# The FFN down products of a streaming trunk step: from fp32r halves to scaled float16 halves

## The chip, the cores and the metric

The kernel runs on one core of one Trainium2 chip, as one program. The metric is the device time of an execution in microseconds; the profile of one execution gives the time of each instruction on TensorE (matmuls and their weight loads), VectorE, ScalarE, GpSimd and on the DMA queues.

## The reference, cut to what matters

One layer (`DEPTH` 1) over 2048 prompt frames and 64 sample frames, 2112 tokens of width 1024: a mixer (gated delta rule and pooling), then a SwiGLU feed-forward network of width 2816, each with a residual addition, and a final norm. The change is about the last product, by `w_down`, and about the operands of it.

```python
def hybrid_layer(x, ...):
    h = rmsnorm(x, norm1_w)
    ...                                   # mixer: o_delta, o_pool and the new states
    x = x + jnp.concatenate([o_delta, o_pool], axis=-1) @ w_out
    h = rmsnorm(x, norm2_w)
    x = x + (jax.nn.silu(h @ w_gate) * (h @ w_up)) @ w_down
    return x, ...
D_FF = -(-8 * D_MODEL // (3 * 256)) * 256   # 2816 = 22 tiles of 128
```

## The kernel before

**Order of the work.** The program writes every operation down in an order of its own; a list scheduler inside it (`Machine`) then simulates the five engines with its own costs and issues each engine's instructions in the order that the simulation found. An operation's rank is its place in the program, lowered by `boost` (`hurry` lowers by `HURRY`, for the operations that read PSUM). The engines run what they were given in that order. Tiles are slots of a tag with a number of buffers, handed out in the simulation; PSUM has eight banks, and the tag "mm" has three (`PSM`). Loads and stores go through SP's queue.

**Mixer.** Four blocks of 512 tokens (the first has the 64 sample frames too), up to about 936 us. Between its weights the plan has steps `("pre", "dn", f0, m)`, 16 of them in blocks 1 to 3: `pre_sums` loads two tiles of `w_down`, forms the Strassen sums on GpSimd, splits each into two fp32r halves and stores them in `dsd`.

**Feed-forward network.** Three blocks of 704 tokens (`NB2`, two halves of `N2` = 352). The 22 f tiles (128 features each) lie in groups of `FGROUPS` = 4, 4, 4, 4, 2, 4. For each block and f tile, `gate_up` makes gate and up as one Strassen product (seven products x, y, z of 12 matmuls, operands as pairs of float16 halves, each product from hi x hi, hi x lo and lo x hi), and leaves silu(gate) * up as a raw tile "hr" of two halves of tokens. Its weights are scaled for each f tile from the data (`scale_of`: sum of squares over the partitions by matmuls of width 1 with ones, then a power of two), split in block 0, stored (`gsd`) and loaded in blocks 1 and 2.

Every second f tile, `factors` makes the seven right factors of the Strassen down product from a pair of raw tiles: four additions on GpSimd (VectorE for the last pair) and seven splits into fp32r halves, a ScalarE cast and a VectorE subtract each, in a tile of tag "op" (two buffers, 13 x 352) and one of tag "h7". `down_strassen` runs a group: for each of four pairs of output tiles m (two for the group of two) seven products of `len(hs)` x 3 matmuls, each added by VectorE into two of the tiles `ys` straight from PSUM. The names of its PSUM tiles in the profile are dx, dy and dz; hq is a factor, wsd and wsdS are weights, wrd the raw weights. Its weights come from `load_down` (sums from `dsd`, the plain quarters loaded raw and split) or, where no sums were stored, from `prep_down` (raw load, sums on GpSimd, four splits). `PRE` says which groups have stored sums in which block.

Plain products, d in the profile, take the place of Strassen's for groups 0 and 4 of block 0 and for the last group of block 2 (the latter in two halves of tokens, so that the last norm can begin); they stay fp32r, before and after, with tiles h3l of the tag "op".

The list `order` says when a group's down work comes: after tile f0 + G for most groups, one tile later for group 0 and, in block 0, for groups 1 to 3 (`LATER`, `LATE0`); for the last group after the last tile. Between the blocks the chain `between` normalises the block just done, loads the next `ys` and makes the next inputs, which `load_h` brings in (hA, hB, hBT).

Of the kernel before, what the change touches and what calls it, by code (L numbers as in the profile page):

```python
# [18 lines left out]
P = 128  # L19
# [33 lines left out]
LATE0 = (1,2,3)  # L53
# [11 lines left out]
class Machine:  # L65
# [124 lines left out]
    def issue(self):  # L190
# [180 lines left out]
def hybrid_kernel(ctx, tc, a, o):  # L371
# [124 lines left out]
    n1w, n2w, nfw = (nw[:, i * KT : (i + 1) * KT] for i in range(3))  # L496
    ones_b = cpool.tile([P, P], BF16, tag="onesb", name="onesb")
# [17 lines left out]
    def weigh_norm():  # L515

        sq = cpool.tile([P, 4], F32, tag="sq", name="sqn", bufs=2)
        junk = cpool.tile([P, KT], F32, tag="junkn", name="junkn")
        act(junk, n2w, AF.Square, accum_out=sq[:, :1])
# [4 lines left out]
    groups, f0 = [], 0  # L524
    for G in FGROUPS:
        groups.append((f0, G))
        f0 += G
    plan, pres = [], []
    for gi, (f0, G) in enumerate(groups):
        pres += [("pre", "gu", f, i) for f in range(f0, f0 + G) if f in PRE_GU for i in range(2)]  # L530
        pres += [("pre", "dn", f0, m) for m in range(KT // 2) if gi in PRE[0]]
# [10 lines left out]
    for j in range(NBLK):  # L542
# [5 lines left out]
        else:  # L548
# [12 lines left out]
    gpd = {(f, i): dpool.tile([4, P, 512], F32, tag=f"gpd{f}_{i}", name=f"gpd{f}_{i}") for f in PRE_GU for i in range(2)}  # L561

# [8 lines left out]
    for b in range(NB2):  # L571
        for f in range(NF):
            order.append(("gu", b, f))
            order += [("dn", b, gi) for gi, (f0, G) in enumerate(groups) if f == min(f0 + G + LATER * (gi == 0 or b == 0 and gi in LATE0), NF - 1)]
    for op in order:
        if op[0] == "gu":
            plan.append(("gu", op[2]))
        else:
            plan += [("dn", m, *groups[op[2]]) for m in range(KT)] * len(halves(*op[1:])) if plain(*op[1:]) else [
                ("ds", m, *groups[op[2]], op[2] in PRE[op[1]]) for m in range(KT // 2 * groups[op[2]][1] // 4)]  # L580
# [16 lines left out]
    def prep():  # L597
        key = plan[state["at"]]
        state["at"] += 1
        if key[0] == "pre":  # L600
            return pre_sums(*key[1:])
        if key in stored and key[0] != "gu":
# [32 lines left out]
        elif key[0] == "ds":  # L635
            parts = load_down(*key[1:4]) if key[4] else prep_down(*key[1:4])
# [4 lines left out]
        while due and due[0][0] != key:  # L641
# [3 lines left out]
            stored.add(k)  # L645

    def prep_strassen(key):
# [16 lines left out]
        junk = wq["pool"].tile([P, 512], BF16, tag="junk", name=f"junk{f}")  # L664
# [28 lines left out]
    def pre_sums(what, f, i):  # L693

        n = 256
        (tl, tr), (ll, lr) = ([t[:, i * n : i * n + n] for i in range(2)] for t in (
            names["poolw"], gp.tile([P, PX], F32, tag="pw", name=f"pr{what}{f}_{i}", bufs=2)[:, :512]))
        if what == "dn":
            for t, m0 in ((tl, i), (ll, i + KT // 2)):
                both = bass.AP(t.tensor, t.offset, [list(t.ap[0]), [1, 2 * n]])  # L700
                nc.sync.dma_start(out=both, in_=a["wd"][m0][:, f * P : f * P + 2 * n])
            dst = dsd[f, i]
        else:
            for t, nm, at in ((tl, "wg", 0), (tr, "wg", 512), (ll, "wu", 0), (lr, "wu", 512)):
                nc.sync.dma_start(out=t, in_=a[nm][f][:, at + i * n : at + i * n + n])
            dst = gpd[f, i]
        gt = nc.gpsimd.tensor_tensor
        spare = B.spare + B.o_spare + (prev.o_spare if prev else [])
# [9 lines left out]
    def split_w(t, x):  # L718

        nc.scalar.copy(t[:, 0], x)  # L720
        tt(t[:, 1], x, t[:, 0].bitcast(F32), ALU.subtract)

    def load_down(m, f0, G):

        n, t = G // 2 * P, {}
        for i, nms in enumerate((("11", "12"), ("S3", "S1"), ("S2", "S4"), ("22",))):
            raw, part = wtiles(f"d{nms[0]}", i % 2 == 1)
            part = part()
            if nms[0][0] == "S":
                both = part.rearrange("p q n -> p (q n)").rearrange("p (j q n) -> p j q n", j=2, q=2)  # L730
                nc.sync.dma_start(out=both.rearrange("p j q n -> p j (q n)").bitcast(F32),
                                  in_=dsd[f0, m][2 * i - 2 : 2 * i].rearrange("j p n -> p j n"))
                t |= {nm: [both[:, j]] for j, nm in enumerate(nms)}
            else:
                raw, k = raw(), n * len(nms)
                src = a["wd"][m + (KT // 2 if i else 0)]
                nc.sync.dma_start(out=raw[:, :k], in_=src[:, (f0 + G) * P - k : (f0 + G) * P])
                wsplit(part, raw, k)
                t |= {nm: [part[:, :, j * n : j * n + n]] for j, nm in enumerate(nms)}
        return t  # L740

    def prep_down(m, f0, G):

        n, M = G // 2 * P, 4 // G
# [3 lines left out]
        for t, m0 in ((top, m * M), (low, m * M + KT // 2)):  # L748
            nc.sync.dma_start(out=parts(t), in_=a["wd"][m0 : m0 + M, :, f0 * P : (f0 + G) * P].rearrange("m p c -> p m c"))
# [6 lines left out]
        t = {}  # L756
        for i, (nms, raw) in enumerate(((("11", "12"), top), (("S3", "S1"), s31), (("S2", "S4"), s24), (("22",), low))):
            part = wtiles(f"d{nms[0]}", i % 2 == 1)[1]()
            if len(nms) == 2:
                wsplit(part, raw)  # L760
            else:
                hi, lo = (part[:, q, : n * M].rearrange("p (m c) -> p m c", m=M) for q in range(2))
                nc.scalar.copy(hi, right(raw))
                tt(lo, right(raw), hi.bitcast(F32), ALU.subtract)
            for j, nm in enumerate(nms):
                t[nm] = [part[:, :, (e * len(nms) + j) * n : (e * len(nms) + j + 1) * n] for e in range(M)]
# [405 lines left out]
    class Head:  # L1172
# [68 lines left out]
        def sample(self):  # L1241
# [30 lines left out]
            f.used = True  # L1272
            osq = yield from self.norm(2 * C, po, qsq)
# [304 lines left out]
    hA = [bp.tile([P, 6, 2, N2], F16, tag=f"h{i}", name=f"hA{i}") for i in range(2)]  # L1578
    for i in range(12):
        hq.setdefault(FH[i // 4], []).append(hA[i // 6][:, i % 6])  # L1580
# [6 lines left out]
    for nm, t in (("dprompt", Sp), ("dsamp", Ss)):  # L1587
# [403 lines left out]
```

## Time and profile before

| what | value |
|---|---|
| time, median of 3 runs | 2258.92 us (2258.83 to 2260.44) |
| profiled execution, its own time | 2261.11 us |
| its span, first to last instruction | 2259.3 us |
| TensorE matmuls busy | 2222.5 us, 14607 instructions |
| VectorE, ScalarE, GpSimd busy | 1639.1, 1358.8, 803.9 us |
| mean granted TensorE clock | 0.997 |
| moved by DMA | 485.01 MB, mean 215 GB/s |

The time is that of an execution on the device; the span runs from the first to the last instruction of the profiled one, 1.8 us less than that execution's own time. A matmul is shown with a modelled end, so busy time and mean length of TensorE overlap from one matmul to the next: the pace is read from starts. A wait is idle time of an engine just before an instruction, with what ended it. All operations are written through one helper, so that every row has the line L285, and groups are told apart by their tiles.

### The profile page before, as it was taken

What the parts mean: (1) busy time and instruction counts of PE and PEld (TensorE: products, weight loads), DVE (VectorE), ACT (ScalarE), POOL (GpSimd) and SP (SyncE); (2) the same over time, 40 slices, a digit from 0 to 9 for tenths busy, and PEclk for the clock granted to TensorE, in tenths of its full rate; (3) what the DMA queues carried; (4) which work ended last, traced back from release to release, by engine and by line L of the source; (5) the groups of instructions that cost most, each with busy time, mean ns of one, the idle gap of its engine ahead of it and who ended that gap; (6) DMA issues with size and microseconds to landing.
All of it is one profiled execution on the core that took longest, in us unless ns stands there. A gap on an engine that the chain in (4) does not pass through costs nothing.

```text
span 2259.3 us, 41012 instructions
## 1 busy us (share of the span) xinstructions
PE 2222.5 (98%) x14607; PEld 1786.3 (79%) x14607; DVE 1639.1 (73%) x3111; ACT 1358.8 (60%) x3131; POOL 803.9 (36%) x893
## 2 busy tenths in 40 slices
PE   8999999999999999999999999999999999999998
PEld 7998898888877888758868778688878778778877
DVE  8988875685568886798888785766656657555565
ACT  6887865685669874796586675653343454442344
POOL 3425442353246551355434236342121353010102
PEclk9999999999999999999999999999999999999999
DMA  8765587568567677885776657578645575556542
GB/s 293 251 208 177 201 277 259 185 226 283 174 231 246 210 190 241 304 284 182 260 266 194 228 204 267 187 242 279 205 139 167 167 262 186 166 164 191 174 144 72
DMA packets 237502, 485.01 MB, mean 215 GB/s; under 512 B 27888, under 2 KB 91888, under 8 KB 237296
## 3 DMA queue, kind: packets, MB, share of 16 engines
q1 hardware_dynamic: 236720, 481.67, 65.1%
q8 instruction: 114, 1.87, 0.3%
q14 instruction: 92, 0.75, 0.1%
q10 hardware_dynamic: 576, 0.72, 0.1%
HBM read 357.48 MB, written 124.81 MB: 213 GB/s over the span
## 4 chain that ended last, share of the span: by engine, by line
PE 86%; DVE 6%; ACT 3%; DMA 2%; issue 1%; POOL 1%; SPq 0%; DVEq 0%; POOLq 0%; ACTq 0%
PE px L285 18%; PE pp L285 17%; PE pz L285 13%; PE dx L285 9%; PE py L285 9%; PE dy L285 5%; PE d L285 3%; PE dz L285 2%; PE pk_p L285 2%; PE pt_p L285 2%; PE gr_p L285 1%; PE py_p L285 1%; DVE y L285 1%; DVE wsS3S L285 0%; DVE hq L285 0%
## 5 line engine op out<-in xcount | busy, mean ns | idle before, releaser
L285 PE MATMUL pp<-h,wsp 128*128 128x512 f32 (+1 forms) x2480 | 547.6, 363 | 10.6 <-DVE wsp L285 10.6
L285 PEld LDWEIGHTS pp<-h,wsp 128*128 128x128 f32 x2480 | 401.1, 189 | 59.0 <-ACT wsp L285 9.6
L285 PEld LDWEIGHTS <-wsS 128*128 128x128 f16 x1584 | 154.2, 98 | 86.4 <-issue 4.5
L285 PEld LDWEIGHTS <-ws11S 128*128 128x128 f16 x1584 | 151.0, 98 | 88.3 <-ACT ws11S L285 3.8
L285 PEld LDWEIGHTS <-wsS3S 128*128 128x128 f16 x1584 | 154.2, 98 | 81.3
L285 POOL TENSOR_TENSOR q<-hr,hr 128x352 f32<-128x352 f32 x52 | 56.5, 1087 | 416.5 <-DVE hr L285 410.7
L285 DVE TENSOR_TENSOR y<-y,dx 128x352 f32<-128x352 f32 x240 | 122.2, 517 | 87.2 <-PE dx L285 86.2
L285 PE MATMUL pz<-op,wsp 128*128 128x288 f32 (+1 forms) x768 | 163.2, 353 | 0.0
L285 ACT CAST wsd<-wrd 128x512 fp32r<-128x512 f32 (+1 forms) x120 | 62.3, 523 | 159.5 <-PE dx L285 64.4
L285 ACT ACTIVATE hr<-g,wscale 128x352 f32<-128x352 f32 x132 | 77.3, 586 | 115.1 <-DVE g L285 115.0
L285 PE MATMUL px<-hA,ws11S 128*128 128x352 f16 x792 | 138.5, 315 | 3.1 <-ACT ws11S L285 2.2
L285 ACT COPY g<-px 128x352 f32<-128x352 f32 x132 | 58.4, 445 | 138.2 <-PE px L285 136.7
L285 ACT CAST TV_p<-pt_p 128x512 f16<-128x512 f32 x192 | 110.3, 589 | 49.8 <-PE pt_p L285 49.4
L285 PE MATMUL dx<-hq,wsd 128*128 128x352 f32 x560 | 137.1, 332 | 2.7 <-ACT wsd L285 2.7
L285 PE MATMUL px<-hA,wsS 128*128 128x352 f16 x792 | 131.6, 315 | 2.5 <-ACT g L285 2.5
L285 PE MATMUL py<-hA,ws11S 128*128 128x352 f16 x792 | 133.7, 313 | 0.3 <-DVE hr L285 0.2
L285 PE MATMUL dx<-hq,wsdS 128*128 128x352 f32 x672 | 132.1, 326 | 1.0 <-DVE hq L285 1.0
L285 PE MATMUL dy<-hq,wsdS 128*128 128x352 f32 x672 | 131.3, 326 | 1.8 <-DVE y L285 1.7
L285 PE MATMUL pz<-hB,wsS 128*128 128x352 f16 x792 | 131.5, 313 | 0.9 <-ACT wsS L285 0.8
L285 PE MATMUL py<-hB,wsS3S 128*128 128x352 f16 x792 | 132.2, 313 | 0.0
L285 PEld LDWEIGHTS pz<-op,wsp 128*128 128x128 f32 x768 | 120.9, 188 | 12.1
L285 PE MATMUL px<-hBT,ws 128*128 128x352 f16 x792 | 129.2, 313 | 1.0 <-DVE u L285 1.0
(739 smaller groups left out, 5367.8 us busy)
## 6 DMA issues: line engine op xcount, KB each, us to landing
wsp<-wnd SPq DMA_DIRECT2D x126, 512.0 KB, 3.9
wsdS<-dsd SPq DMA_DIRECT2D x88, 512.0 KB, 4.0
ws11S<-g SPq DMA_DIRECT2D x44, 512.0 KB, 4.4
wsS<-g SPq DMA_DIRECT2D x44, 512.0 KB, 4.4
wsS3S<-g SPq DMA_DIRECT2D x44, 512.0 KB, 4.4
wnd<-wsp SPq DMA_DIRECT2D x42, 512.0 KB, 5.1
wrd<-in_wd_dram SPq DMA_DIRECT2D x68, 256.0 KB, 2.8
xd<-x2d SPq DMA_DIRECT2D x96, 176.0 KB, 3.9
```

The costliest lines, as they stand in the source:

```text
L285: getattr(getattr(self.nc, op.eng), name)(*args, **kw)
```

## The change

The operands of the Strassen down products become pairs of float16 halves, as those of gate and up already are, so that values have to be scaled. Each group of f tiles gets one power of two for its activations (`factors`): `gate_up` sums the squares of every raw half (`esq`), and once the group's last tile is there, `scale_of` adds them over the partitions and the halves are split with that scale (`split16`). `factors` therefore runs once for a group instead of once for a pair, and down work of groups 0 to 3 comes one tile after the next group's first, that of groups 4 and 5 after the last tile (`LATER`, `LASTD`). Weights get a scale for each pair of output tiles (`down_scale`); both are taken out where the product is added to `ys`, by a scalar `inv`. Weight halves are stored in `dparts` at their first use and only loaded after that: sums in the mixer by `pre_sums` (now after the sample state is stored, since its tile is the staging buffer), the plain quarters in block 0, groups 0 and 4 in block 1. The tag "hr" has 7 buffers instead of 3, "op" holds a whole group's factors in the same bytes, six of the seven input factors lie in hA. In the scheduler, from the FFN on, a PSUM tile that isn't first in its queue can't take the last free slot.

The diff, cut; "@@" names the function.

```diff
-LATE0 = (1,2,3)
@@ serve
+            if nm and nm is not q[0] and len(self.slots[tag]) < 2 and self.parked[nm][0].order > self.second:
+                return
@@ scale_of
-    def scale_of(out, squares, n, top, ps):
-        cols = cpool.tile([P, 4], BF16, tag="sqb", name=f"sqb{machine.n}", bufs=2)[:, :n]
-        nc.vector.tensor_copy(cols, squares)
+    def scale_of(out, squares, n, top, ps, tag="sqb"):
+        cols = (cpool if tag == "sqb" else wq["pool"]).tile([P, 8], BF16, tag=tag, name=f"{tag}{machine.n}", bufs=2)[:, :n]
+        nc.vector.tensor_copy(cols, squares[:, :n])
         for i in range(n):
             mm(ps[:, :1], ones_b, cols[:, i : i + 1], start=i == 0, stop=i == n - 1)
@@ where the halves are stored
-    dsd = {(f0, m): dpool.tile([4, P, 512], F32, tag=f"dsd{f0}_{m}", name=f"dsd{f0}_{m}")
-           for f0, G in (groups[gi] for gi in PRE[0]) for m in range(KT // 2 * G // 4)}
+    dparts = {(f0, m): [dpool.tile([P, w], F16, tag=f"dn{i}_{f0}_{m}", name=f"dn{i}_{f0}_{m}") for i, w in enumerate((2048, 1536))]
+              for f0, G in groups for m in range(KT // 2 * G // 4)}
@@ order
-            order += [("dn", b, gi) for gi, (f0, G) in enumerate(groups) if f == min(f0 + G + LATER * (gi == 0 or b == 0 and gi in LATE0), NF - 1)]
+            order += [("dn", b, gi) for gi, (f0, G) in enumerate(groups) if f == (min(f0 + G + LATER, NF - 1) if gi < LASTD else NF - 1)]
@@ prep
         if key[0] == "pre":
+            if not state.get("sampled"):
+                return plan.insert(next(i for i in range(state["at"], len(plan)) if plan[i][0] != "pre") + 1, key)
             return pre_sums(*key[1:])
...
-            parts = load_down(*key[1:4]) if key[4] else prep_down(*key[1:4])
+            parts = prep_down(key, *key[1:])
@@ new helpers
+    def two_squares(name, top, low, junk):
+        sq = cpool.tile([P, 4], F32, tag="sq", name=f"sq{name}", bufs=2)
+        for i, x in enumerate((top, low)):
+            act(junk, x, AF.Square, accum_out=sq[:, i : i + 1])
+        return sq
+    def down_scale(f, m, sq):
+        i = dindex[f, m]
+        scale_of(dscale[:, 0, i : i + 1], sq, 2, 2.0**13, psp.tile([P, 512], F32, tag="mm", name=f"wd{f}_{m}", bufs=PSM))
+        nc.vector.reciprocal(dscale[:, 1, i : i + 1], dscale[:, 0, i : i + 1])
+        return dscale[:, 0, i : i + 1]
+    def split16(hi, lo, x, scale):
+        act(hi, x, AF.Copy, scale=scale)
+        stt(lo, x, scale, hi, ALU.mult, ALU.subtract)
@@ pre_sums
+        stage = names["sdelta"].bitcast(F16)
+        scale = down_scale(f, m, two_squares(f"p{f}_{m}", *whole, stage.bitcast(BF16)[:, :512]))
         gt = nc.gpsimd.tensor_tensor
...
-        for j, x in enumerate((ll, lr, tl, tr)):
-            parts = spare[j % len(spare)]
-            split_w(parts.rearrange("p (q n) -> p q n", q=2), x)
-            nc.sync.dma_start(out=dst[j], in_=parts.bitcast(F32))
+        for j, (two, parts) in enumerate((((ll, lr), stage), ((tl, tr), pr.bitcast(F16)))):
+            both = parts.rearrange("p (q n) -> p q n", q=2)
+            for k, x in enumerate(two):
+                split16(*(both[:, q, k * n : k * n + n] for q in range(2)), x, scale)
+            nc.sync.dma_start(out=dparts[f, m][j][:, 1024 * (1 - j) : 1024 * (2 - j)], in_=parts)
@@ prep_down (load_down is gone)
+        if key in stored:
+            for part, src in zip(flat16, kept):
+                nc.sync.dma_start(out=part[:, : src.shape[-1]], in_=src)
+            return t
+        if (f0, m) in summed:
...
+            nc.sync.dma_start(out=flat16[0][:, 1024:], in_=kept[0][:, 1024:])
+            nc.sync.dma_start(out=flat16[1][:, :1024], in_=kept[1][:, :1024])
+            for part, src, k, second in ((quad[0], a["wd"][m], 512, False), (quad[3], a["wd"][m + KT // 2], 256, True)):
...
+                split16(part[:, 0], part[:, 1], raw[:, :k], scale)
+            due.append((key, [(kept[0][:, :1024], flat16[0][:, :1024]), (kept[1][:, 1024:], flat16[1][:, 1024:1536])]))
+            return t
...
+        scale = down_scale(f0, m, two_squares(f"d{f0}_{m}", top, low, junk16()))
...
+            split16(hi, lo, raw, scale)
+        due.append((key, list(zip(kept, (flat16[0], flat16[1][:, :1536])))))
@@ sample
+            nc.sync.dma_start(out=o["dsamp"].rearrange("h k v -> k h v"), in_=Ss)
+            state["sampled"] = True
@@ FFN inputs
-    hA = [bp.tile([P, 6, 2, N2], F16, tag=f"h{i}", name=f"hA{i}") for i in range(2)]
+    hA = [bp.tile([P, 12, 2, N2], F16, tag=f"h{i}", name=f"hA{i}") for i in range(2)]
@@ gate_up
+            if not plain(b, gi):
+                k = 2 * (f - groups[gi][0]) + i
+                act(junk16()[:, :N2], e, AF.Square, accum_out=esq[b, gi][:, k : k + 1])
@@ factors
-    def factors(b, f, u, v):
-        t = opool.tile([P, 13, N2], F32R, tag="op", name=f"hq{b}_{f}", bufs=2)
-        low = f2.tile([P, N2], F32R, tag="h7", name=f"h7{b}_{f}", bufs=2)
+    def factors(b, gi):
+        f0, G = groups[gi]
+        es = einv[b, gi] = f2.tile([P, 6], F32, tag="es", name=f"es{b}_{gi}", bufs=2)
+        c = es[:, :1]
+        scale_of(c, esq.pop((b, gi))[:, : 2 * G], 2 * G, 2.0**13, psp.tile([P, 512], F32, tag="mm", name=f"ec{b}_{gi}", bufs=PSM), "sqe")
+        nc.vector.reciprocal(es[:, 1:2], c)
+        t = opool.tile([P, 13 * G // 2, N2], F16, tag="op", name=f"hq{b}_{gi}", bufs=2)
+        for p in range(G // 2):
...
+            for nm, x in (("11", u[:, 0]), ("21", v[:, 0]), ("22", v[:, 1])):
+                split16(*part[nm], x, c)
...
+            for nm, x in (("T1", u[:, 1]), ("T2", t2), ("T3", t3), ("T4", t4)):
+                split16(*part[nm], x, c)
+            h3[f] = part
@@ down_strassen
+            i, inv = dindex[f0, m], einv[b, gi][:, 2 + m : 3 + m]
+            ts(inv, dscale[:, 1, i : i + 1], einv[b, gi][:, 1:2], None, ALU.mult)
...
-                    hurry(tt, out, out, ps, ALU.add)
+                    hurry(stt, out, ps, inv, out, ALU.mult, ALU.add)
@@ the main loop
-                elif f % 2:
+                elif f == sum(groups[gi]) - 1:
                     machine.boost = HURRY if f == NF - 1 else 0
-                    h3[f] = factors(b, f, h3.pop(f - 1), h3[f])
+                    factors(b, gi)
-LATER = 1
+LATER, LASTD = 1, 4
+HRAW = 7
```

## Rows read from the trace of the kernel before

**Rows 1.** The chain that ended last: share of the span by engine.
```profile
PE 86%; DVE 6%; ACT 3%; DMA 2%; issue 1%; POOL 1%; SPq 0%; DVEq 0%; POOLq 0%; ACTq 0%
```

**Rows 2.** Busy time by stage: stretch, length, busy (instructions), clock, DMA share.
```profile
0.00:936.00 936.00, 921.70 (x6127) 786.28 (x6127) 708.78 (x1443) 663.41 (x1634) 381.59 (x503) 1.00 0.71 230
936.00:1392.00 456.00, 444.36 (x2917) 339.55 (x2918) 389.44 (x697) 317.92 (x709) 195.43 (x161) 0.99 0.70 240
1392.00:1806.00 414.00, 411.33 (x2677) 314.63 (x2676) 268.18 (x479) 186.72 (x395) 127.75 (x130) 1.00 0.62 199
1806.00:2217.00 411.00, 411.00 (x2689) 313.61 (x2688) 247.49 (x450) 172.62 (x360) 85.24 (x88) 1.00 0.57 180
```

**Rows 3.** TensorE's waits from 930 to 1310 us: sum, times, longest.
```profile
PE dx L285 <- ACT wsd L285: 2.7, 1, 2.7
PE px L285 <- ACT g L285: 2.5, 3, 1.9
PE px L285 <- ACT ws11S L285: 2.2, 3, 1.3
```

**Rows 4.** TensorE's waits from 1310 us to the end.
```profile
PE dy L285 <- DVE y L285: 1.7, 1, 1.7
PE dx L285 <- DVE hq L285: 1.0, 1, 1.0
```

**Rows 5.** Busy time and granted clock just after those two waits.
```profile
1798.00:1801.00 3.00, 2.48 (x8) 2.48 (x9) 3.00 (x8) 0.86 (x3) 1.67 (x2) 0.52 0.81 244
```

**Rows 6.** TensorE's groups from 930 us: count, busy us, mean ns, idle before.
```profile
L285 PE MATMUL dx<-hq,wsd 128*128 128x352 f32 x560 | 137.1, 332 | 2.7 <-ACT wsd L285 2.7
...
L285 PE MATMUL dx<-hq,wsdS 128*128 128x352 f32 x672 | 132.1, 326 | 1.0 <-DVE hq L285 1.0
...
L285 PE MATMUL dy<-hq,wsdS 128*128 128x352 f32 x672 | 131.3, 326 | 1.8 <-DVE y L285 1.7
...
L285 PE MATMUL dz<-hq,wsd 128*128 128x352 f32 x336 | 71.2, 326 | 0.4 <-DVE g L285 0.4
...
L285 PE MATMUL dx<-h,wsd 128*128 128x352 f32 x112 | 36.2, 323 | 0.0
...
L285 PE MATMUL ws<-sqb,onesb 128*128 128x1 bf16 x88 | 5.0, 165 | 0.0
```

**Rows 7.** Timeline of TensorE: down products, first and last of six rows.
```profile
1975.87 1.12 PE L285 MATMUL dx<-hq,wsdS 128*128 128x352 f32 x6
...
1980.70 0.96 PE L285 MATMUL dz<-hq,wsd 128*128 128x352 f32 x5
```

**Rows 8.** Timeline of TensorE: gate/up products, first and last of five rows.
```profile
2070.87 1.95 PE L285 MATMUL px<-hBT,wsS3S 128*128 128x352 f16 x12
...
2078.03 1.95 PE L285 MATMUL py<-hA,ws11S 128*128 128x352 f16 x12
```

**Rows 9.** Weight loads from 930 us: count, busy us, mean ns.
```profile
L285 PEld LDWEIGHTS <-wsS 128*128 128x128 f16 x1584 | 154.2, 98 | 86.4 <-issue 4.5 <-DVE wsS L285 0.4
...
L285 PEld LDWEIGHTS dx<-hq,wsdS 128*128 128x128 f32 x672 | 112.1, 189 | 2.0 <-DVE hq L285 1.3
```

**Rows 10.** Timeline of TensorE: one set of scale matmuls.
```profile
1161.86 0.24 PE L285 MATMUL ws<-sqb,onesb 128*128 128x1 bf16 x4
```

**Rows 11.** VectorE's groups by form, 930 us to the end.
```profile
L285 DVE TENSOR_TENSOR y<-y,dx 128x352 f32<-128x352 f32 x240 | 122.2, 517 | 87.2 <-PE dx L285 86.2
...
L285 DVE SCALAR_TENSOR_TENSOR hr<-hr,wscale,px 128x352 f32<-128x352 f32 x66 | 38.1, 578 | 41.2 <-PE px L285 40.8
```

**Rows 12.** ScalarE's groups by form, 930 us to the end.
```profile
L285 ACT ACTIVATE hr<-g,wscale 128x352 f32<-128x352 f32 x132 | 77.3, 586 | 115.1 <-DVE g L285 115.0
...
L285 ACT CAST hq<-hr 128x352 fp32r<-128x352 f32 x112 | 52.8, 485 | 45.5 <-DVE hr L285 35.7 <-PE dx L285 6.0 <-POOL hr L285 2.1
...
L285 ACT ACTIVATION_READ_ACCUMULATOR junk<-gr 128x1 f32 x33 | 6.2, 187 | 0.0
...
L285 ACT ACTIVATE sq4nf<-y 128x352 f32<-128x352 f32 x6 | 3.0, 496 | 0.7 <-DVE y L285 0.4 <-POOL rf L285 0.3
```

More of the change, by code (lines that the diff above doesn't have):

```diff
@@ L496, in hybrid_kernel @@
     n1w, n2w, nfw = (nw[:, i * KT : (i + 1) * KT] for i in range(3))
+    groups, f0 = [], 0
+    for G in FGROUPS:
+        groups.append((f0, G))
+        f0 += G
     ones_b = cpool.tile([P, P], BF16, tag="onesb", name="onesb")
@@ L502, in hybrid_kernel @@
     wscale = []
-    def scale_of(out, squares, n, top, ps):
-        cols = cpool.tile([P, 4], BF16, tag="sqb", name=f"sqb{machine.n}", bufs=2)[:, :n]
-        nc.vector.tensor_copy(cols, squares)
+    dindex = {}
+    for f0, G in groups:
+        for m in range(KT // 2 * G // 4):
+            dindex[f0, m] = len(dindex)
+    dscale = cpool.tile([P, 2, len(dindex)], F32, tag="dscale", name="dscale")
+    def scale_of(out, squares, n, top, ps, tag="sqb"):
+        cols = (cpool if tag == "sqb" else wq["pool"]).tile([P, 8], BF16, tag=tag, name=f"{tag}{machine.n}", bufs=2)[:, :n]
+        nc.vector.tensor_copy(cols, squares[:, :n])
         for i in range(n):
@@ L645, in prep, with junk16 @@
             stored.add(k)
+    def junk16():
+        return wq["pool"].tile([P, 512], BF16, tag="junk", name=f"junk{machine.n}")
     def prep_strassen(key):
@@ L663, in prep_strassen @@
         sq = cpool.tile([P, 4], F32, tag="sq", name=f"sq{f}", bufs=2)
-        junk = wq["pool"].tile([P, 512], BF16, tag="junk", name=f"junk{f}")
+        junk = junk16()
         for i, (nm, src) in enumerate((("11", "11"), ("S1", "21"), ("22", "22"), ("12", "12"))):
@@ L691, in prep_strassen, with pre_sums @@
         return t
-    def pre_sums(what, f, i):
-        n = 256
[L696 to L706, printed above, removed]
+    def two_squares(name, top, low, junk):
[11 more added lines that the diff above has]
+        stt(lo, x, scale, hi, ALU.mult, ALU.subtract)
+    def pre_sums(f, m):
+        n = 256
+        pr = gp.tile([P, PX], F32, tag="pw", name=f"pr{f}_{m}", bufs=2)[:, :512]
+        (tl, tr), (ll, lr) = ([t[:, i * n : i * n + n] for i in range(2)] for t in (names["poolw"], pr))
+        whole = []
+        for t, m0 in ((names["poolw"], m), (pr, m + KT // 2)):
+            nc.sync.dma_start(out=t, in_=a["wd"][m0][:, f * P : f * P + 2 * n])
+            whole.append(t)
+        stage = names["sdelta"].bitcast(F16)
+        scale = down_scale(f, m, two_squares(f"p{f}_{m}", *whole, stage.bitcast(BF16)[:, :512]))
         gt = nc.gpsimd.tensor_tensor
-        spare = B.spare + B.o_spare + (prev.o_spare if prev else [])
         gt(out=lr, in0=lr, in1=ll, op=ALU.add)
@@ L755, in prep_down @@
         gt(out=right(s24), in0=right(top), in1=left(s24), op=ALU.subtract)
[L756 to L760, printed above, removed]
-            else:
[L762 to L766, printed above, removed]
+        for part, raw in zip(quad, (top, s31, s24, right(low))):
+            if raw.shape != part[:, 0].shape:
+                hi, lo = (parts(part[:, q]) for q in range(2))
+            else:
+                hi, lo = part[:, 0], part[:, 1]
+            split16(hi, lo, raw, scale)
+        due.append((key, list(zip(kept, (flat16[0], flat16[1][:, :1536])))))
         return t
@@ L1595, in hybrid_kernel @@
     banks += [("mm", PSM), ("bk", 1), ("mm", PSM), ("bo", 1), ("mm", PSM)] + [(f"b{i}", 1) for i in range(NLEV)]
-    for nm in FH[3:]:
-        t = f2.tile([P, 4, 2, N2], F16, tag=f"h{nm}", name=f"hB{nm}")
-        hq[nm] = [t[:, k] for k in range(4)]
+    hB = f2.tile([P, 4, 2, N2], F16, tag="hB", name="hB")
+    hq[FH[6]] = [hB[:, k] for k in range(4)]
     fill = Chain(load_h(0, FH[3:]))
@@ L1627, in new @@
         def new(nm):
-            return f2.tile([P, 2, N2], F32, tag="hr", name=nm, bufs=3).rearrange("p s n -> p (s n)")[:, :n] if n > N2 else tmp(nm)[:, :n]
+            return f2.tile([P, 2, N2], F32, tag="hr", name=nm, bufs=HRAW).rearrange("p s n -> p (s n)")[:, :n] if n > N2 else tmp(nm)[:, :n]
         rf = new(f"rf{b}_{i}")
         if i:
-            scaled, scales = [], f2.tile([P, 2, N2], F32, tag="hr", name="scales", bufs=3).rearrange("p s n -> p (s n)")
+            scaled, scales = [], f2.tile([P, 2, N2], F32, tag="hr", name="scales", bufs=HRAW).rearrange("p s n -> p (s n)")
         for k in range(KT):
@@ L1680, in gate_up @@
         six = b == 0 and gi < min(STR0)
-        raw = f2.tile([P, 2, N2], F32, tag="hr", name=f"hr{tag}", bufs=3)
+        raw = f2.tile([P, 2, N2], F32, tag="hr", name=f"hr{tag}", bufs=HRAW)
+        if f == groups[gi][0] and not plain(b, gi):
+            esq[b, gi] = f2.tile([P, 8], F32, tag="esq", name=f"esq{tag}", bufs=2)
         def add(ps, nw, nh, first=False):
```

91 lines of the change are left out of this document (34 added, 57 removed).

## The prediction

> **What bounds the kernel now.** I read the chain that ended last first: 86% of the span lies on TensorE [rows 1], so the time is the sum of what TensorE issues plus what it waits for. Second, the busy times by stage [rows 2]: the mixer up to 936 us, then the three FFN blocks. TensorE is shown busy almost throughout, and that view doesn't separate a full engine from one that hops between short waits; the waits do that. Third, therefore, TensorE's waits: in block 0 it is idle 11.6 of 456 us [rows 2], mostly for ScalarE, the longest waits being those of [rows 3]; in blocks 1 and 2 together 2.7 us [rows 2], all at the turn from block 1 to block 2 [rows 4], where the granted clock fell too: 0.52 over 3 us [rows 5], so nearly all of that stretch ran at 1.2 GHz, the lower of TensorE's two levels, after the two waits. Everything else in blocks 1 and 2 is issue. A cheaper matmul there is a shorter block, and VectorE (268 of 414 us, 247 of 411) and ScalarE (187, 173) have room for work. In block 0 VectorE is busy 389 of 456 us: little room.
>
> **Term 1: the pace of the down products.** The Strassen down products are the groups dx, dy and dz: 560 + 672 + 672 + 336 + 112 = 2352 matmuls of 128x352, all fp32r (the view writes f32) [rows 6]. A group of four f tiles is 4 x 7 x 6 = 168 of them, the two-tile group 84: 672 in block 0 (four groups of four), 924 in block 1, 756 in block 2. Their pace is start to start, not the 320 ns shown as length: from 1975.87 to 1980.70 there start 30, so 161.0 ns each [rows 7]. The gate/up products are the same shape in float16: from 2070.87 to 2078.03 there start 48, so 149.2 ns each [rows 8]. Difference 11.8 ns, times 2352: **-27.8 us** (-7.9, -10.9 and -8.9 by block). Both paces are of stretches without a wait; waits that the quicker pace brings out are term 5 and the rivals.
>
> The weight loads differ with the type as well: 189 ns for fp32r, 98 ns for float16 [rows 9]. The Trainium skill (TensorE: Matmul & The Clock Gate, section Weight-path perf modes) says that the array takes one element per cell and cycle whatever the element's width, and that a weight load goes by columns and not by bytes; by that fp32r and float16 of one shape would pace alike and term 1 would be 0, the sum +3.9 instead of -23.9. The trace disagrees on both, 161.0 against 149.2 ns and 189 against 98; the measurement decides, and the rule is kept as rival (d).
>
> **Term 2: matmuls added for the scales.** A group's activation scale sums 2G columns, one matmul of width 1 per column: 13 groups of four give 8 each, two groups of two give 4, so 112. Weight scales take 2 each: 16 in the mixer, 6 in block 1 (groups 0 and 4), so 44. The same kind is in the trace, in fours: ws<-sqb, four within 0.24 us [rows 10], of which the last one's own length of 165 ns [rows 6] is the tail, so about 25 ns from start to start. 156 of them: **+3.9 us**. The upper bound is the whole length for each, 26 us, which the row of four excludes; zero is the lower.
>
> **Term 3: the two-tile group is moved.** Group 4's down work is now issued after the last gate/up tile, not before it. In block 1 that puts 84 matmuls, 84 x 0.149 = 12.5 us, between the last gate/up and group 5's products. Today group 5 starts at once, and TensorE waits for VectorE's halves hq and for y, 1.0 + 1.7 us [rows 4], then runs about 3 us at clock 0.52, which costs half of them, 1.5 [rows 5]. In the new order group 5 needs, after the last gate/up: square, copy, matmuls of width 1, two ScalarE steps, mask, reciprocal, one split; at 0.2 to 0.7 us each some 4 us, under the 12.5 of cover. **-4 us** (bounds -4.2, and 0 if the two pairs' halves, now in one batch, are late again). Without the cover those 4 us would be lost instead. In block 0 group 4 is plain and that turn shows no wait: 0.
>
> **Term 4: block 2's end.** The last group's plain halves sit in tiles of the two-deep tag "op". Group 4's factors now hold one of the two until group 4's products have ended, so the second plain tile (f 20 and 21) is split only then: four times a ScalarE cast (0.485) and a VectorE subtract (like y's, 0.517) [rows 11, 12]. Plain matmuls over f 18 and 19, six for each output tile, can run ahead of them. I take **+1 us** (bounds 0, and 2.5 for four splits in a row with no cover).
>
> **Term 5: work on the other engines.** ScalarE gets 112 squares with a sum, 496 + 187 ns each, 76 us, and 196 factor halves as a scaled copy (586, like hr<-g) instead of a cast (485), 20 us [rows 12]; it loses the casts of the down weights that blocks 1 and 2 now load as halves, 80 of them at some 0.5, 40 us. VectorE's 420 additions into y take a scale: 578 ns (the form hr<-hr,wscale,px, which reads PSUM too) instead of 517 [rows 11], +26 us; 196 low halves take the same 0.06 more, +12; 80 weight subtracts are gone, 40 us. So in blocks 1 and 2 VectorE has less to do and ScalarE some 30 us more over 825. Block 0, which still splits weights, gets about 31 us more on ScalarE (318 of 456 now) and 17 more on VectorE (389 of 456) [rows 2]. This is hidden where no wait ends on it. But each group's scale is a chain across three in-order engines: the ScalarE step that waits for the width-1 matmul holds up the copies of gate/up results queued behind it, and TensorE waits for those. Today's 22 such chains, one for each gate/up tile of block 0, go with waits of TensorE on ScalarE's g, 2.5 us, and ws11S, 2.2 [rows 3]: 0.2 us a chain. For 15 new ones **+3 us** (bounds 0, and 15 x 1.9, the longest such wait, = 28); nearer to the mean than to the longest, since 11 of them lie in the emptier blocks.
>
> **Costed at nothing.** The mixer's 16 weight sums each get two squares of 512, two ScalarE steps and three tiny ones on VectorE, in all about 40 us of ScalarE and 11 of VectorE; the cover is the 936 us in which ScalarE is busy 663 and VectorE 709 [rows 2] while TensorE has independent matmuls; bounds -2 and +3. SP's queue loses about 512 KB of loads for each down weight, gains stores of 384 KB for each in block 0 and of 896 KB at six places of block 1, and the sample state's store is issued earlier; the DMA engines are 0.57 to 0.70 busy [rows 2], so a late load has slack. The rule on the last PSUM slot bites only when one slot of three is left. The deeper buffer of raw h only frees; the extra gate/up tile between factors and products of groups 1 to 3 (blocks 1, 2) gives 12 us of cover.
>
> **Sum.** -27.8 + 3.9 - 4 + 1 + 3 = -23.9. The profiled execution took 2261.1 us, 2.2 above the median of 2258.9: 2237.2 for it, **2235 us** as a median. By stage: block 0 448 to 451, block 1 400 to 402, block 2 403 to 405 us.
>
> **Rivals.**
> (a) *The scale chains take the gain.* If each of the 15 costs the longest ScalarE wait, 1.9 us [rows 3], term 5 is 28 and the time 2260; with a clock that falls after each as at the turn (1.5 more [rows 5]) 2282. Longer than before from 1.8 us a chain. For it: three in-order engines, and the factors of two pairs now queue on GpSimd at once. Against: 0.2 a chain today, in the fuller block. Chance 0.06.
> (b) *Block 0 becomes VectorE's.* 389 of 456 us busy, 17 added: if that block follows VectorE, its gain of 7.9 goes and up to 9 are added: 2243 to 2252. For it: 85% busy [rows 2]. Against: the longest of TensorE's waits there end on ScalarE [rows 3]. Chance 0.17.
> (c) *Block 0's waits go too.* The wait for wsd, 2.7 us [rows 3], and part of the other copies' are dealt anew: -5, and the chains cost nothing, -3: 2227. Chance 0.1.
> (d) *Width doesn't matter.* Term 1 is 0, the rest gives +3.9: 2263. Chance 0.02; 161.0 against 149.2 speaks against it [rows 7, 8]. It is what the rule of TensorE: Matmul & The Clock Gate (the Trainium skill), section Weight-path perf modes, would make of the change.
> The sum itself, within about 7 us: 0.65.
>
> **Range and chances.** A measurement of this kernel can't tell less than 0.2% (2254.4 to 2263.4) from no change. From (c), less a little, to the far end of (b): **2224 to 2250**, which leaves out (a), (d) and edges. Faster by over 0.2%: the sum, (c) and (b), 0.91. Same: (d), a mild (a), 0.04. Slower: (a) in full, 0.05.
>
> **What would show it.** dx, dy and dz as f16 matmuls, 2352 of them, starting every 149 ns: term 1; at 160, wrong. Sets of width 1 at 25 ns: term 2. No wait of TensorE for hq or y at the turn from block 1 to 2, the clock whole there: term 3. A wait for h3l before the last plain products: term 4. TensorE waiting for ScalarE's g or a group's halves in blocks 1 and 2: rival (a). Block 0 above 452 us with waits that end on VectorE: rival (b). The prediction is wrong if a block doesn't shorten by its count of down products.

## The result, and the profile after

The changed kernel takes 2267.53 us (median of 13 runs, 2265.14 to 2272.4) beside 2260.54 for the kernel before, run with it (13 runs): ratio 1.0032, interval 1.0024 to 1.0041. The forecast was 2235, range 2224 to 2250; it is 0.3% slower instead of 1% faster.

TensorE's stretches first, cut at events that both kernels have: the first gate/up matmul, and the last Strassen down product of each block (columns as in [rows 2]).

```profile
0.00:942.00 942.00, 924.86 (x6159) 789.82 (x6159) 709.46 (x1494) 692.92 (x1730) 374.35 (x503) 1.00 0.68 220
942.00:1395.00 453.00, 435.95 (x2941) 297.90 (x2942) 396.50 (x722) 344.65 (x789) 204.97 (x167) 0.99 0.71 240
1395.00:1830.00 435.00, 423.98 (x2839) 275.22 (x2837) 264.87 (x521) 214.95 (x504) 119.49 (x130) 0.98 0.63 199
1830.00:2223.00 393.00, 390.13 (x2642) 256.32 (x2641) 211.92 (x415) 167.09 (x381) 53.29 (x58) 1.00 0.50 156
```

In the mixer TensorE's and VectorE's busy numbers hardly differ from before (ScalarE is busy 30 us more). In block 1 (third row) TensorE is idle 11 of 435 us at a clock of 0.98. The kernel before, cut at the same events, was idle 2.7 of 431 there:

```profile
1391.00:1822.00 431.00, 428.33 (x2785) 330.00 (x2783) 276.46 (x496) 193.85 (x411) 138.01 (x142) 1.00 0.64 207
```

The products themselves did as foreseen; the timeline of a stretch without waits in block 2:

```profile
1982.63 0.61 PE L286 MATMUL dx<-hq,wsd 128*128 128x352 f16 x3
...
1987.55 0.31 PE L286 MATMUL dy<-hq,wsd 128*128 128x352 f16 x1
...
1989.34 0.91 PE L286 MATMUL dz<-hq,wsd 128*128 128x352 f16 x5
```

From 1982.63 to 1989.34 there start 45, 149.1 ns each, beside the 161.0 of [rows 7]; all 2352 are f16 now. So the gain was made and lost again. By stretch (table below) the three blocks together are 1.6 us shorter than before and the mixer is 6.7 longer. Where the blocks lost it, TensorE's waits from 1310 us to the end say (sum, times, longest):

```profile
PE dz L286 <- DVE y L286: 3.2, 2, 2.6
PE ec L286 <- DVE sqe L286: 3.1, 1, 3.1
PE dx L286 <- ACT wsd L286: 2.8, 1, 2.8
PE dy L286 <- DMA out_yT_dram<-y: 1.6, 1, 1.6
PE px L286 <- DVE u L286: 1.5, 1, 1.5
PE dx L286 <- ACT hq L286: 1.4, 1, 1.4
...
PE dx L286 <- DVE y L286: 0.7, 1, 0.7
PE dx L286 <- DVE hq L286: 0.6, 1, 0.6
```

Before, the same stretch had two waits of 1 us or more, 1.7 and 1.0 [rows 4]. Most of the new ones end on VectorE or on an engine that waited for it. Most of their time lies in three places: the two turns between blocks, and block 1's first group (1460 to 1486 us, 5.5 us in all, the wait for wsd among them). Take first the turn from block 1 to block 2, the one that term 3 had freed of its wait. VectorE there (timeline; "x4" are four in a row):

```profile
1781.65 1.07 DVE L286 SCALAR_TENSOR_TENSOR y<-dx,es,y 128x352 f32<-128x352 f32 x2
1782.64 1.07 DVE L286 SCALAR_TENSOR_TENSOR y<-dy,es,y 128x352 f32<-128x352 f32 x2
...
1793.95 0.58 DVE L286 SCALAR_TENSOR_TENSOR y<-dy,es,y 128x352 f32<-128x352 f32 x1
1794.44 0.58 DVE L286 SCALAR_TENSOR_TENSOR hr<-hr,wscale,g 128x352 f32<-128x352 f32 x1
1795.05 0.58 DVE L286 SCALAR_TENSOR_TENSOR hr<-hr,wscale,u 128x352 f32<-128x352 f32 x1
...
1797.54 0.16 DVE L286 CAST sqe<-esq 128x8 bf16<-128x8 f32 x1
...
1798.85 0.16 DVE L286 RECIPROCAL es<-es 128x1 f32<-128x1 f32 x1
...
1799.54 2.06 DVE L286 SCALAR_TENSOR_TENSOR hq<-hr,es,hq 128x352 f16<-128x352 f32 x4
1801.52 1.07 DVE L286 SCALAR_TENSOR_TENSOR hq<-q,es,hq 128x352 f16<-128x352 f32 x2
...
1803.01 1.57 DVE L286 SCALAR_TENSOR_TENSOR hq<-hr,es,hq 128x352 f16<-128x352 f32 x3
```

From 1781.65 to 1794.44 it adds group 4's products into y, 26 additions in 12.8 us, and only then finishes the last raw tile (hr). ScalarE's squares wait for that, then the cast to sqe, the sum on TensorE, the scale es, and then all the group's halves at once. TensorE, in the same stretch:

```profile
1793.60 0.31 PE L286 MATMUL dx<-hq,wsd 128*128 128x352 f16 x1 [0.70 <-DVE y L286]
...
1797.75 0.34 PE L286 MATMUL ec<-sqe,onesb 128*128 128x1 bf16 x8 [3.06 <-DVE sqe L286]
1799.48 1.04 PE L286 MATMUL dx<-hq,wsd 128*128 128x352 f16 x3 [1.39 <-ACT hq L286]
...
1802.37 0.50 PE L286 MATMUL dy<-hq,wsd 128*128 128x352 f16 x1
1802.66 0.50 PE L286 MATMUL dx<-hq,wsd 128*128 128x352 f16 x1
1802.95 0.50 PE L286 MATMUL dy<-hq,wsd 128*128 128x352 f16 x1
```

It waits 0.70, 3.06 and 1.39 us, and then starts its matmuls 0.29 us apart, which is half the pace: the granted clock of the last two rows below is 0.62 over 9 us and 0.50 from 1800 to 1805, the lower of its two levels, 1.2 GHz. At the turn from block 0 to block 1 it is the same with another last link: fourteen low halves occupy VectorE from 1356 to 1366 us, and the first of six additions y<-y,d behind them ends dz's wait of 2.65 us.

```profile
1366.18 2.66 DVE L286 TENSOR_TENSOR y<-y,d 128x352 f32<-128x352 f32 x6
1366.74 1.92 PE L286 MATMUL dz<-hq,wsd 128*128 128x352 f16 x6 [2.65 <-DVE y L286]
```

Busy time in stretches about the turns (the first row is the turn from block 0 to block 1):

```profile
1360.00:1368.00 8.00, 4.32 (x23) 2.51 (x23) 8.00 (x14) 6.38 (x14) 6.04 (x7) 0.81 0.89 284
...
1781.00:1797.00 16.00, 12.76 (x83) 7.96 (x82) 15.77 (x32) 1.54 (x5) 0.00 (x0) 1.00 0.53 173
1797.00:1806.00 9.00, 6.85 (x33) 3.75 (x33) 8.90 (x25) 7.62 (x18) 0.00 (x0) 0.62 0.29 93
1800.00:1805.00 5.00, 5.00 (x18) 2.58 (x17) 5.00 (x12) 5.00 (x11) 0.00 (x0) 0.50 0.33 97
```

Of TensorE's clock the Trainium skill (TensorE: Matmul & The Clock Gate, section What's actually happening) says that the throttled state is the default and that there are only two states, no level between. On the levels these rows agree: but for a single matmul at each change the pace is 0.149 or 0.29 us, and 0.62 is a mean over a stretch with both.

### The profile page after: what moved, and what is told of

Its sections match the earlier page's. It is cut to its first block, busy times and chain, and to the rows that moved or that the text cites. A ratio compares the mean times of both kernels' runs of the same rounds, so it can differ in the third digit from the quotient of the medians.

```text
span 2264.0 us, 41509 instructions
## 1 busy us (share of the span) xinstructions
PE 2207.0 (97%) x14763; PEld 1649.5 (73%) x14763; DVE 1611.4 (71%) x3198; ACT 1437.4 (63%) x3437; POOL 767.0 (34%) x869
## 5 line engine op out<-in xcount | busy, mean ns | idle before, releaser
L286 PEld LDWEIGHTS <-wsd 128*128 128x128 f16 x2352 | 231.1, 99 | 143.1 <-issue 13.7
L286 PE MATMUL dx<-hq,wsd 128*128 128x352 f16 x1232 | 237.6, 316 | 9.5 <-ACT wsd L286 2.8
L286 DVE SCALAR_TENSOR_TENSOR y<-dx,es,y 128x352 f32<-128x352 f32 x240 | 135.3, 579 | 72.7 <-PE dx L286 68.2
L286 PE MATMUL pz<-hA,wsS 128*128 128x352 f16 x792 | 134.4, 313 | 0.9 <-ACT wsS L286 0.8
L286 PE MATMUL py<-hA,wsS3S 128*128 128x352 f16 x792 | 134.3, 312 | 0.1
L286 PE MATMUL dy<-hq,wsd 128*128 128x352 f16 x672 | 129.7, 319 | 3.3 <-DMA out_yT_dram<-y 1.6
L286 PE MATMUL px<-hB,ws 128*128 128x352 f16 x792 | 129.5, 313 | 2.0 <-DVE u L286 2.0
L286 PE MATMUL px<-hA,wsS3S 128*128 128x352 f16 x792 | 129.6, 313 | 0.7 <-ACT g L286 0.6
```

The lines of the kernel that those rows point to most:

```text
L286: getattr(getattr(self.nc, op.eng), name)(*args, **kw)
```

## The experiments

All but e11, e12 are the changed kernel with the edit shown. Each ratio is to the kernel before, run beside it on the same chip. Differences in us are between medians; the kernel before took 2260.2 to 2262.8 us on the chips of these runs, so such a difference is known to some 2 us. Every edit also makes the scheduler deal the instructions anew, so the waits in the traces have to show the cause beside the times. The theory after the traces: the activations' scale makes all halves of a group wait for its last tile, and the burst behind it is what TensorE waits for. Rivals: the moved group 4, the work of squares and chains by itself, the dearer additions, the weights' scales. The letters in the expectations stand for what is said there with them.

**e1: group 4 back to its old place.**

```diff
-LATER, LASTD = 1, 4
+LATER, LASTD = 1, 5
```

> Group 4's down work goes back before the last gate/up tiles (after tile 19); all else as in the changed kernel (2267.5 us, against 2260.5 before). Theory A, VectorE at the turns: between the last gate/up tile and group 5's products VectorE has to make 28 additions of 0.58 us for group 4, issued ahead of the last tile's own finish, and so group 5's factors come late; without them the waits at the two turns (4.2 and 6.0 us, and some 1.8 us each at the lower clock) become a bare chain of 3 to 5 us: 3 to 8 us shorter. Theory B, the scale chains: the chain is as long as before and now has no cover: the turns wait 5 us or more each, no gain or up to 5 us longer.

Measured 2269.5 us, ratio 1.0043 (1.0028 to 1.0058): no shorter, as theory B has it. At the turns TensorE now waits 3.9 and 3.6 us before the sums ec and 1.4 each for hq, without cover. The moved group alone isn't the cause.

**e2: a constant for the activations' scale.** Left out: the squares, their sum, the scale chain. `csc` holds the constants 64 and 1/64.

```diff
-                act(junk16()[:, :N2], e, AF.Square, accum_out=esq[b, gi][:, k : k + 1])
+                pass
...
-        c = es[:, :1]
-        scale_of(c, esq.pop((b, gi))[:, : 2 * G], 2 * G, 2.0**13, ...)
-        nc.vector.reciprocal(es[:, 1:2], c)
+        c = csc[:, :1]
```

> The activation scale is the constant 64: the squares of the raw halves, the width-1 matmuls ec, the two ScalarE steps, mask and reciprocal of each group are left out; halves, stored weights and order stay. Theory B, the scale chains: the waits that end on them go (3.1 and 1.4 us at the turn from block 1 to 2) and block 0's too: 8 to 12 us shorter, under the time before. Theory A: the last tile's finish is still queued behind group 4's additions and the products wait for their halves instead: 3 us shorter or less, most of it at the turn.

2236.26 us, 0.989 (0.9876 to 0.9905): 31.3 less than the changed kernel, far more than either theory gave. That the total is the forecast's 2235 is luck: by the table below block 0 is 13.7 us shorter than before, where the pace gives 7.9 (the wait of 2.7 for wsd in [rows 3] is gone too), and the mixer is 10 longer.

**e3: a constant for the weights' scale.** Left out: the squares of the down weights, their sums and chains. `wsc` holds the constants 4096 and 1/4096.

```diff
     def down_scale(f, m, sq):
...
         i = dindex[f, m]
-        scale_of(dscale[:, 0, i : i + 1], sq, 2, 2.0**13, ...)
-        nc.vector.reciprocal(dscale[:, 1, i : i + 1], dscale[:, 0, i : i + 1])
-        return dscale[:, 0, i : i + 1]
+        return wsc[:, :1]
```

> The weight scale is the constant 4096: the two squares, the matmuls wd, two ScalarE steps, mask and reciprocal are left out for each down weight, 16 times in the mixer and 6 times in block 1. Theory B: block 1's group 0 loses the wait on the scaled halves of its weights (2.8 + 0.7 us and the slow clock behind them), 5 to 6 us, and the mixer, 5.9 us more of waits than before, comes back to about 927 us from the first to the last matmul: 10 us shorter in all. Theory A: block 1's group 0 waits for y, which is late anyway, and the mixer's waits are of the order in which its chains were dealt: 3 us shorter or less.

2263.75 us, 1.0012 (1.0003 to 1.0022): 3.8 less. The mixer's stretch is 930.8 us beside 933.6 in the changed kernel; block 1 is no shorter (436.3). In its first group the wait for wsd is gone, and waits for VectorE stand in its place:

```profile
PE dz L286 <- DVE hr L286: 3.6, 1, 3.6
PE dz L286 <- DVE y L286: 3.4, 1, 3.4
```

**e4: the addition without its factor.** The sum into y leaves `inv` out, so it is a plain addition again (517 instead of 578 ns).

```diff
-                    hurry(stt, out, ps, inv, out, ALU.mult, ALU.add)
+                    hurry(tt, out, out, ps, ALU.add)
```

> The products are added to y without the factor that takes the scales out (so the output is scaled wrongly): a plain addition of 0.52 us in place of one with a multiplication of 0.58, 420 times, 26 us of VectorE. Theory A: VectorE sets the turns and block 0, so 5 to 8 us shorter, most of it in block 1 and at the turns. Theory B: within 3 us of the changed kernel.

2260.95 us, 0.9995 (0.9986 to 1.0005): 6.6 less. A quarter of the 26 us of VectorE time that the factor adds comes out in the end. Block 1 is 4.6 us shorter (430.8) and block 0 3.0 (449.3), the blocks with the waits for VectorE: where it sets the pace, its time counts.

**e5 and e6: the work without the dependence, and the dependence without the work.** In e5 squares, sums and chain are made as before, but the halves are split with a constant, so nothing waits for them. In e6 the halves still wait for the last tile, but its scale comes from one square of the last half alone; 97 of the 112 squares and their columns in the sum are left out.

```diff
 e5
-                split16(*part[nm], x, c)
+                split16(*part[nm], x, csc[:, :1])
...
 e6
-                act(junk16()[:, :N2], e, AF.Square, accum_out=esq[b, gi][:, k : k + 1])
+                if i == 0 and f == sum(groups[gi]) - 1:
+                    act(junk16()[:, :N2], e, AF.Square, accum_out=esq[b, gi][:, :1])
...
-        scale_of(c, esq.pop((b, gi))[:, : 2 * G], 2 * G, 2.0**13, ...)
+        scale_of(c, esq.pop((b, gi))[:, :1], 1, 2.0**11, ...)
```

> The group scale is computed as in the changed kernel (112 squares, 15 chains with their width-1 matmuls), but the halves are split with the constant 64 and don't wait for it. Theory C, the work: the squares on ScalarE and the chain's place in three in-order queues cost the 31 us that the constant gave back, so about as slow as the changed kernel, 2260 to 2270 us. Theory D, the dependence: all 28 halves of a group of four may start only when its last tile is squared and summed, so they come in one burst; with the constant each can be split as soon as its tile is there, and this kernel is near 2236 us, at most 5 above.

> The group scale comes from the last half of the last tile alone: one square and one width-1 matmul for each group instead of 8, the wait of all halves for it as in the changed kernel. Theory C, the work: most of it is gone, 2236 to 2245 us. Theory D, the dependence: it is all there, 2258 to 2268 us.

e5: 2244.18 us, 0.9933 (0.9917 to 0.9949). e6: 2258.42 us, 0.9992 (0.9983 to 1.0001). Without the dependence 23.4 of the 31.3 go (theory D allowed e5 5 us above e2, and it is 8); without the work 9.1. The two add up: 22 to 23 us are the wait for the group's last tile, 8 to 9 the work. Of e5's 8 above e2, 6 lie in block 0, the fullest one (446.5 beside 440.4). There TensorE waits in its own order at the width-1 matmuls ec, whose result nothing waits for in e5 (950 to 1310 us):

```profile
PE ec L286 <- ACT wscale L286: 4.3, 2, 3.0
```

**e7: a scale known before the group.** The group's scale comes from the scales of its gate and up weights, which are there long before: the least over its tiles, squared, times a constant. No squares, no sum over the partitions, no wait for the last tile.

```diff
-                act(junk16()[:, :N2], e, AF.Square, accum_out=esq[b, gi][:, k : k + 1])
+                pass
...
-        scale_of(c, esq.pop((b, gi))[:, : 2 * G], 2 * G, 2.0**13, ...)
+        s = wscale[0][:, 0, f0 : f0 + G]
+        nc.vector.tensor_reduce(out=c, in_=s, axis=mybir.AxisListType.X, op=ALU.min)
+        ts(c, c, c, 2.0**-12, ALU.mult, ALU.mult)
```

> The group scale is worked out from the gate/up weight scales of its tiles (the least of them, squared, by a constant), which are known from block 0's weight preparation on: three small VectorE steps for each group, no squares, no matmuls, no wait for activations. By theories C and D alike within 3 us of the constant's 2236 us, faster than both kernels by 1%; if something else in the constant's kernel gave the time, up to 2268.

2236.73 us, 0.9898 (0.9881 to 0.9914): 1% faster than the kernel before, with scales that still come from data, those of the weights; they no longer follow the size of the activations. The turn from block 1 to 2 in its timeline, VectorE:

```profile
1760.76 0.58 DVE L286 SCALAR_TENSOR_TENSOR h<-q,es,hq 128x352 f16<-128x352 f32 x1
...
1764.40 1.07 DVE L286 SCALAR_TENSOR_TENSOR y<-dx,es,y 128x352 f32<-128x352 f32 x2
1765.38 0.57 DVE L286 SCALAR_TENSOR_TENSOR hq<-hr,es,hq 128x352 f16<-128x352 f32 x1
...
1779.71 0.58 DVE L286 SCALAR_TENSOR_TENSOR hr<-hr,wscale,g 128x352 f32<-128x352 f32 x1
...
1782.50 0.58 DVE L286 SCALAR_TENSOR_TENSOR hq<-hr,es,hq 128x352 f16<-128x352 f32 x1
...
1783.43 0.58 DVE L286 SCALAR_TENSOR_TENSOR hq<-q,es,hq 128x352 f16<-128x352 f32 x1
```

The additions are there as before, and the last tile's finish (hr, 1779.71) is as far behind them. But the first pair's seven low halves are done with the row at 1760.76, before the additions; of the second pair's, one is made at 1765.38 among them, and only the last five come after the last tile, in turn with the sums q. The waits of TensorE from 1750 to 1830 us are one row:

```profile
PE dy L286 <- DVE hq L286: 0.3, 1, 0.3
```

**e8: both scales constant.** The edits of e2 and e3 together.

> Both scales are constants (64 and 4096): no squares, sums or scale steps in the down products at all, halves, stored weights and order as in the changed kernel. The weight scale alone gave 4 us, the activation scale 31. If the two are independent, 2231 to 2234 us; if block 1's waits were one and the same, 2236. The mixer, 927 us from first to last matmul before and 934 to 937 with the weight scale, comes back to 927 if the scale steps are all that slowed it, and stays at 931 if the other staging buffers do part of it.

2229.41 us, 0.9866 (0.9851 to 0.9881): 6.9 below e2; its expectation had 2 to 5 us, or none. The mixer, 929.9, comes back only in part.

**e9 and e10: where the wait costs.** The constant of e2 in groups 4 and 5 alone (the turns between blocks), and in groups 0 to 3 alone.

```diff
 e9 (e10: gi < 4)
-            if not plain(b, gi):
+            if not plain(b, gi) and not (gi > 3):
...
-        c = es[:, :1]
+        c = csc[:, :1] if gi > 3 else es[:, :1]
```

> Leaves out the data's activation scale (squares, sum, chain) in groups 4 and 5 alone, which take the constant 64; groups 0 to 3 keep theirs. Theory D (the halves of a group wait for its last tile and then come in one burst) with the place at the turns: what the two turns lose goes, by the profile after some 6 at block 0 to 1 and 7 at block 1 to 2, so about 2254 +- 3. Rival E (the loss is spread over all groups' bursts): 5 of 13 scaled groups are changed, so 5/13 of the 31 that the constant scale gave: 2255.5 by time alone, but then blocks 0, 1 and 2 shorten by like parts and the waits for hq, sqe and y at the turns stay above half of what they are. What tells them apart is e10's part and the stretches 1360 to 1368 and 1780 to 1803.

> Leaves out the data's activation scale in groups 0 to 3 alone (constant 64); groups 4 and 5, at the turns, keep theirs. Theory D at the turns: the turns' 13 stay, block 0 (its groups 1 to 3) and the first groups of blocks 1 and 2 give back the rest of 31, so about 2250 +- 4. Rival E: 8/13 of 31, 2248. Rival F (only the turns matter): 2266.

e9: 2254.37 us, 0.9967 (0.9957 to 0.9977), 13.2 less. e10: 2247.46 us, 0.9942 (0.9926 to 0.9959), 20.1 less. Together 33.3, about e2's 31.3. That the time goes by place is seen in the waits: e9 has none over 0.2 us from 1340 to 1400 us and one, 0.3, from 1750 to 1830; e10 has kept both turns: at the first 2.1, 0.6 and 0.4 us, and at the second (1750 to 1830 us, the two longest):

```profile
PE ec L286 <- DVE sqe L286: 3.1, 1, 3.1
PE dx L286 <- ACT hq L286: 1.8, 1, 1.8
```

By time alone rival E, an equal loss for each group, would do for both; the waits that vanish in e9 while block 1's first ones stay (wsd, 2.6 us) speak for the places. In e10 it is the other way: no wait of block 1's first group is over 0.9 us, with the weights' scales untouched, so that place too depends on the activation scale.

**e11: e7 with group 4 in its old place**, the edit of e1 made in e7.

> The scale from the gate and up weights (no wait for the data's squares) with group 4's down work issued one tile earlier, as before the change. The prediction's term 3 (its products cover the last group's halves, 4 us): 2241. Rival G (its 28 additions cost VectorE as long as its products take TensorE, so the place makes no difference once halves can be made tile by tile): 2237 +- 2.

2238.99 us, 0.9908 (0.9889 to 0.9927), e7 0.9898 (0.9881 to 0.9914): the intervals overlap, so the place of the group is worth at most some 2 us and perhaps nothing. By stretch, block 1 is 419.2 us here and 419.0 in e7.

**e12: the kernel before with late sums.** Only the lines that put off the mixer's weight sums until the sample part has ended.

```diff
         if key[0] == "pre":
+            if not state.get("sampled"):
+                return plan.insert(next(i for i in range(state["at"], len(plan)) if plan[i][0] != "pre") + 1, key)
             return pre_sums(*key[1:])
...
+            state["sampled"] = True
```

> The kernel before, with only the mixer's weight sums put off until the sample part has ended, as the change does; nothing else is changed and nothing is left out. If the delay makes the 3 us by which the mixer stays longer even with both scales constant: mixer 930 and 2263. If it is something else (the staging tile, the schedule dealt anew): mixer 927 and 2260.

2269.05 us, 1.0038 (1.0025 to 1.0051): 8 us slower than the kernel before, and its mixer is 9.2 longer, with the same work; neither expectation held. The delay was not even a term of the sum.

The stretches of the profiled executions, worked out from the starts of TensorE's matmuls, in us:

| kernel | mixer | block 0 | block 1 | rest |
|---|---|---|---|---|
| before | 926.9 | 454.1 | 430.8 | 429.5 |
| after | 933.6 | 452.3 | 435.4 | 425.1 |
| e2, activations constant | 937.0 | 440.4 | 419.1 | 420.7 |
| e5, scale not waited for | 938.6 | 446.5 | 422.3 | 421.4 |
| e6, last half only | 934.1 | 449.8 | 432.9 | 422.6 |
| e7, scale from the weights | 933.7 | 442.2 | 419.0 | 420.5 |
| e8, both constant | 929.9 | 440.2 | 422.3 | 420.5 |
| e9, constant at the turns | 937.6 | 445.5 | 426.3 | 424.6 |
| e10, constant in groups 0 to 3 | 933.6 | 445.8 | 426.8 | 420.9 |
| e12, before, late sums | 936.1 | 452.9 | 431.2 | 429.5 |

In the mixer TensorE has the same matmuls in the same order in after, e2, e5, e6, e7, e9 and e10, and still takes 933.6 to 938.6: one profile tells a mixer to some 2.5 us either way. (Where VectorE, ScalarE and GpSimd have the same order too, in after, e1, e4, e6, e7 and e11, it took 933.6 to 935.4.)

## Why the prediction was wrong, by its own steps

**Term 1, -27.8, held.** All 2352 are float16, and away from waits the pace is 149.1 against 161.0 ns. Taking out of each stretch what TensorE's matmuls start later than the median of their kind (a first fp32r matmul behind a float16 one, which starts early, taken with the next), blocks 0 and 1 and the rest go from some 434.9, 425.6 and 427.3 us to 427.6, 416.2 and 419.3: -24.7, in which terms 1 and 2 stand together (-23.9, or -24.7 without the 0.8 that term 2 puts into the mixer). Rival (d) falls.

**Term 2, +3.9, held.** In the trace the eight ec matmuls at the turn to block 1 take 0.21 us from the first start to the next product's, 26 ns each.

**Term 5, +3, is the step that failed, and term 3 with it.** Measured, the activation scale costs 31 us (e2), beside +3 and bounds of 0 to 28. The step priced a chain by today's, one late ScalarE copy, 0.2 us each. But those chains are of weights that are loaded ahead; TensorE waits for few of them (ws11S, three times [rows 3]). A group's activation scale stands before the very next products: fourteen ScalarE copies and fourteen VectorE halves, which the kernel before made pair by pair, can begin only when the last tile is squared and summed, and come in one burst. That order is 22 to 23 of the 31 (e5, e6), the squares and chains themselves 8 to 9 (e5 against e2). "Room for work", read from VectorE's 268 busy of 414 us, was a mean over a stage whose loss lies at its two ends and in its first group.

**Term 3, -4,** took group 4's 12.5 us of products for cover. On VectorE their additions start 0.49 us apart, and there is one for every three matmuls of 0.149, that is for 0.45 us of TensorE: the cover kept VectorE full for 12.8 us (rows from 1781.65) and put the last tile's finish behind it. "Some 4 us, under the 12.5 of cover" counted the chain from the last gate/up matmul; it began 13 us later. Once the scale doesn't wait (e7, e11) the place of the group makes no difference that shows. The turns together cost 13 (e9): waits of 3.7 us at the first, which the step had put at 0, and some 5 at the second, and after them sixteen and nineteen matmuls at half the pace, 2.3 and 2.7.

**Term 4, +1:** no wait for h3l is among those after 2150 us, where the only one is 0.2 for rf. It was 0 to TensorE.

**The factor in the additions,** hidden by the sum's account, was not all hidden: 6.6 us (e4), measured with the bursts in place, so part of the same 31.

**Costed at nothing: the mixer.** -2 to +3 was said, and the stretch grew by 6.7 in the two profiles. e3 and e8 take back 2.8 and, against e2, 7.1 with constant weight scales. e12 shows that the delay of the sums, without any of the new work, makes the mixer 9.2 longer in the kernel before: presumably because other work falls on the same engines at other times, which no run shows. But e3 and e8 have the delay too, and their mixers are only 3 to 4 longer than before. How much of the changed kernel's 6.7 is the delay stays open: a kernel with another staging tile, with which the sums could stay early, was not tried.

**The rivals.** (a) had the right place, "a group's halves in blocks 1 and 2", and its total, 2260 to 2282, holds the result; its mechanism, a ScalarE step that holds up gate/up copies, is not what the trace of the changed kernel shows (TensorE's waits for g sum to 2.7 us in block 0, as 2.5 before), and 0.06 was far too little. (b) named VectorE, but for block 0 alone; block 0 did lose most of its gain (452.3), to the activation scale, since it is 440.4 in e2: in part to the same bursts (446.5 in e5), in part to the squares and chains.

## What to carry to other kernels

A scale taken from the data of a whole group makes everything that uses it wait for the group's last piece: price not only the chain but the burst of work released behind it, on every engine that must do it before the next product. A scale from something known earlier (here the weights' scales, e7) keeps the gain, 1% here. And work counts as cover for another engine's chain only if that chain's engines are not busy with the cover's own results.

## What was not expected of the hardware

After the waits at the two turns, 3.7 and some 5 us, TensorE ran its next sixteen and nineteen matmuls 0.29 us apart instead of 0.149, at a granted clock of 0.50: the waits cost over half as much again as they lasted. And the same matmuls in the same order took 933.6 to 938.6 us in the mixer in seven programs, 0.5%, while the median of the kernel before was 2260.2 to 2262.8 us on the four occasions, 0.1%.
